# Reordering the first output projection of a two-block kernel, and issuing S5's transfers from GpSimd's queue

## The chip, the cores and the metric

One core of one Trainium2 chip runs the whole program. The metric is device time in microseconds, the median of three executions: 3645.99 us for the kernel before (3644.5 to 3646.58).

## The reference, cut to what matters

Two transformer-like blocks run on 256 tokens of width 2048, in float32. The change touches only the first half of the first block:

```
z = rmsnorm(x) @ w_in;  q, k, v, o, gates, u = split(z)
q, k = silu(causal_conv4(q, k))
hm = headnorm(mlstm(q, k, v, gates)) * g * sigmoid(o)     # 4 heads of 256: 1024 columns
ys = s5(u)             # 64 groups of 16 with a complex state of 64, gelu, 16x32 matrix per group, gate
x  = x + concat(hm, ys) @ w_out                           # 2048 x 2048
```

The S5 part is computed in chunks of 8 tokens: taps (the 8 by 8 kernel of a chunk), inputs (what a chunk adds to the state), a scan over 32 chunks, and outputs (state part plus taps part). The rest of the kernel (a PEER layer, then the second block) is untouched.

## The kernel before, in words

Every matrix product (`gemm`, L247 to L276) streams its weights from HBM: SyncE's queue loads 512 KB into `raw` (L238, 4 buffers), ScalarE writes the rounded high part `wh` (L247), VectorE the rest `wl` (L248), and TensorE does three matmuls for each block of 128 rows and each half of the tokens (L274 to L276) into a pair of PSUM banks `g`. There are four `g` banks, so two tiles of 512 columns are open at once. A second PSUM pool of four banks, `b`, serves all small products and transposes (L308 is the transposing helper).

Side work is written as Python generators in three queues (`side`). After each raw load, `gemm` calls `step`, which advances each queue by `steps` yields. Queue 0 holds S5, queue 1 the gates, heads 0 and 2 of mLSTM and the output gate `fin`, queue 2 heads 1 and 3. So the program order of S5 against the big product is set by counting yields. The tile framework then schedules each engine's stream by a model of its own, with program order as the priority; buffers are handed out by pool.

`phase_a` runs the stage. The first three column tiles of `w_in` give u and the gates, with one step for each of their 18 loads; S5's parameters (12 yields) and its first taps (7 yields) use them up but for one step. Then come eight tiles of 512 columns with 8 loads each and two steps a load, 16 steps a tile: v, q, k, output gate for heads 0 and 1 (half 0), then the same for half 1. The callback of a v tile copies it out to `V1` (L806, one buffer), that of a q or k tile copies it to `ev` (L813, two buffers), transposes it through `b` banks, copies it into `zp` (L815, one buffer) and convolves it (ACT L820, VectorE L822), then applies SiLU (L824). After k of a half its two heads are queued.

S5 (`s5_all`) takes, in steps: 5 for `s5_put_u` (u goes to DRAM and comes back regrouped as `U`, 8 transfers of 128 KB, L497), 7 for each of three further `s5_taps`, 4 for each of four `s5_in`, 15 for `s5_states` (the scan on GpSimd, L540 to L543), 6 for each of four quarters of `s5_out` (it begins by loading the quarter's taps, 1 MB, from DRAM into the only `s5t0` buffer, L554; its matmuls are L576 and L582; it draws two `b` banks in its fifth step and one in its sixth), and 8 for each `s5_glu`, which follows one quarter later (8 writes to DRAM at L599, one read back as `yT` at L603, six yields, then two steps with a `b` bank and two matmuls L610 each). All those transfers are on SyncE's queue, among the raw loads.

After the eight tiles, `w_out` runs in two passes of four column tiles: first its rows 1024 to 2047 against S5's half (`mix[1]`, in the buffers `s5t0` and `s5b`), adding to X; then, after draining the side queues, rows 0 to 1023 against mLSTM's half (`mix[0]` in `s5q`, filled by `mix_hm`), adding to X, transposing X into `xh` and `xl` for the next stage (`put_T`) and storing it.

```python
            self.gemm("w_out", [512] * 4, KD, *mix[1], cb_1, steps=2, ks=(8, 16))
            self.drain()
            self.gemm("w_out", [512] * 4, KD, *mix[0], cb_2, ks=(0, 8))
```

Of the kernel before, what the change touches and what calls it, by code (L numbers as in the profile page):

```python
# [11 lines left out]
F32 = mybir.dt.float32  # L12
F32R = mybir.dt.float32r
# [136 lines left out]

class Kern:
    def __init__(self, tc, A, ctx):
        self.tc, self.nc, self.A, self.ctx = tc, tc.nc, A, ctx
        self.side = [[], [], []]
        self.GB, self.heads = {}, set()
        self.raw_slots, self.raw_n = [None], 0
        self.half_step = []
# [22 lines left out]
    def drain(self, qs=(0, 1, 2)):  # L180
# [170 lines left out]
    def s5_params(self, p):  # L351
# [86 lines left out]
        nc.sync.dma_start(self.Kd.rearrange("q h s c -> (q h) s c")[:, 0:7, :],  # L438
# [4 lines left out]
    def s5_taps(self, p, q):  # L443
# [38 lines left out]
        nc.sync.dma_start(dr.rearrange("p g o -> p (g o)"), self.A["s5d"][:, q * 256:(q + 1) * 256])  # L482
# [3 lines left out]
        nc.sync.dma_start(bass.AP(tensor=k.tensor, offset=k.offset + q * 16 * 3840 + 7 * 256,  # L486
# [3 lines left out]
    def s5_put_u(self, p, uT):  # L490

        nc = self.nc
        ud = self.dram.tile([8, 128, 256], F32, name="ud")
        nc.sync.dma_start(ud.rearrange("n p x -> p n x"), uT.rearrange("p n j c -> p n (j c)"))
# [52 lines left out]
    def s5_out(self, p, q, yg):  # L547
# [4 lines left out]
        t0 = p.tile([128, 8, 16, 16], F32, name="s5t0")  # L552
        k = self.Kd
        nc.sync.dma_start(t0.rearrange("p i g o -> p (i g o)"),  # L554
                            bass.AP(tensor=k.tensor, offset=k.offset + q * 16 * 3840,
                                    ap=[[256, 8], [3840, 16], [1, 2048]]))
# [35 lines left out]
    def s5_glu(self, p, q, yg, ys):  # L592

        nc, V = self.nc, self.nc.vector
# [23 lines left out]
    def s5_all(self, p, uT, ys):  # L618
        yield from self.s5_put_u(p, uT)
        self.glu = p.tile([128, 8, 2, 128], F32, name="s5c")  # L620
        self.nc.sync.dma_start(self.glu.rearrange("p a b c -> p (a b c)"), self.A["glu"])
# [124 lines left out]
    def phase_a(self):  # L746
        nc, V, A = self.nc, self.nc.vector, self.A
        with ExitStack() as ex:
# [46 lines left out]
            def cb(i, P):  # L795
# [29 lines left out]
                if kind:  # L825
                    for h in range(2):
                        self.add_side(self.mlstm_head(mp, half * 2 + h, cur[1], cur[2], cur[0], hm), 1 + h)

            def fin(half, og):
                while not {2 * half, 2 * half + 1} <= self.heads:  # L830
                    yield
                for tb in range(2):
                    z = hm[tb][:, half * 512:(half + 1) * 512]
                    V.tensor_tensor(z, z, og[:, tb], op=OP.mult)
                yield
# [3 lines left out]
            X = [self.xx.tile([128, D], F32, name=f"X{tb}") for tb in range(2)]  # L839
            for tb in range(2):  # L840
                nc.sync.dma_start(X[tb], A["x"][tb * 128:(tb + 1) * 128, :])
            xh = self.act.tile([128, KD, T], F32R, name="xh")
            xl = self.act.tile([128, KD, T], F32R, name="xl")
            mix = [[s5.tile([128, 8, T], F32R, name=n, bufs=2 if n == "s5q" else 1) for n in nn]
                   for nn in (("s5q", "s5q"), ("s5t0", "s5b"))]
            for q in range(4):
                k, y = slice(2 * q, 2 * q + 2), ys[:, 2 * q:2 * q + 2]
                h, l = (z[:, k] for z in mix[1])
                nc.scalar.activation(h, y, AF.Copy)
                V.tensor_tensor(l, y, h.bitcast(F32), op=OP.subtract)  # L850

            def mix_hm():
                for q in range(2):
                    for tb in range(2):
                        z = hm[tb][:, q * 512:(q + 1) * 512]
                        b = self.transpose4([z[:, n * 128:(n + 1) * 128] for n in range(4)])
                        t = slice(tb * 128, tb * 128 + 128)
                        for n in range(4):
                            k = q * 4 + n
                            g = self.vecs[:, 48 + k:49 + k]  # L860
                            bn = b[:, n * 128:(n + 1) * 128]
                            h, l = (z[:, k, t] for z in mix[0])
                            nc.scalar.activation(h, bn, AF.Copy, scale=g)
                            V.scalar_tensor_tensor(l, bn, g, h.bitcast(F32), op0=OP.mult, op1=OP.subtract)
                        yield
            self.add_side(mix_hm(), 1)


            ss = self.xx.tile([128, 2, 4], F32, name="mss")

            def cb_1(i, P):
                for tb in range(2):
                    xs = X[tb][:, i * 512:(i + 1) * 512]
                    V.tensor_tensor(xs, xs, P[tb], op=OP.add)

            def cb_2(i, P):
                cb_1(i, P)
# [886 lines left out]
```

## Time and profile before

| what | value |
|---|---|
| median of 3 executions | 3645.99 us |
| profiled execution, its own time | 3642.74 us |
| its span, first to last instruction | 3641.0 us |
| TensorE busy | 3562.5 us, 98% of the span |
| granted TensorE clock, mean | 0.992 of full speed |

A span is taken from the first to the last recorded instruction. "PE" is TensorE's matmuls, "PEld" its weight loads, DVE is VectorE, ACT ScalarE, POOL GpSimd, SP SyncE. A row's releaser, after the arrow, is what ended the idle time ahead of the instruction. A granted clock of 1.00 is 2.4 GHz, 0.5 is 1.2 GHz.

### The profile page before, as it was taken

To read this page: it belongs to the slowest core of one execution; us is meant where nothing else is said; L and a number is where in the kernel's file an instruction comes from. 1 tells how busy PE (TensorE), PEld (TensorE's weight loads), DVE (VectorE), ACT (ScalarE), POOL (GpSimd) and SP (SyncE) were. 2 spreads that over 40 slices of the span, in tenths; PEclk is the share of its full clock that TensorE was granted. 3 is DMA by queue.
4 is the path that set the end of the run, shared out by engine and by line. 5 is a ranking of instruction groups with operands and counts; after the bars stand their busy time and mean duration, and the time that the engine had idled before them with its cause. 6 is when DMAs were issued, how large, how long until landed. Compare 5 with 4: busy or idle time off the path is not lost.

```text
span 3641.0 us, 52884 instructions
## 1 busy us (share of the span) xinstructions
PE 3562.5 (98%) x17442; PEld 2957.0 (81%) x17442; DVE 2711.8 (74%) x5655; ACT 2010.5 (55%) x3511; POOL 485.4 (13%) x645
## 2 busy tenths in 40 slices
PE   9898999999999999999999999999999999999999
PEld 7676888788888788888888788888887888888888
DVE  8685779869999977777777877766777666666554
ACT  6455655555555555555555666774454555555443
POOL 1060000014455500001000100000111000000000
PEclk9998999999999999999999999999999999999999
DMA  7656555555555578888887555466886577776565
GB/s 208 179 166 152 184 176 178 180 180 172 177 166 167 168 256 287 284 287 319 288 284 261 182 168 158 146 202 202 285 294 217 163 231 226 233 227 217 188 195 162
DMA packets 228516, 766.07 MB, mean 210 GB/s; under 512 B 40529, under 2 KB 44497, under 8 KB 226193
## 3 DMA queue, kind: packets, MB, share of 16 engines
q1 hardware_dynamic: 197728, 647.89, 56.0%
q0 software_dynamic: 30512, 114.81, 10.0%
q8 instruction: 137, 2.24, 0.2%
q14 instruction: 139, 1.13, 0.1%
HBM read 753.23 MB, written 9.37 MB: 209 GB/s over the span
## 4 chain that ended last, share of the span: by engine, by line
PE 77%; DVE 2%; POOL 1%; DMA 1%; issue 1%; ACT 1%; DVEq 0%; ACTq 0%; POOLq 0%
PE g L276 18%; PE g L274 18%; PE g L275 18%; PE g L1115 3%; PE g L1117 3%; PE b L1116 3%; PE b L1115 3%; PE g L1116 3%; PE b L1117 3%; PE b L308 1%; PE b L1064 1%; DVE wl L248 0%; POOL e L1057 0%; PE b L1456 0%; DMA fg<-in_fg_row 0%
## 5 line engine op out<-in xcount | busy, mean ns | idle before, releaser
L247 ACT ACTIVATE wh<-raw 128x512 fp32r<-128x512 f32 (+2 forms) x2068 | 1290.3, 629 | 1273.4 <-PE g L275 656.3
L248 DVE TENSOR_TENSOR wl<-raw,wh 128x512 fp32r<-128x512 f32 (+2 forms) x2068 | 1436.0, 705 | 663.4 <-ACT wh L247 613.3
L274 PE MATMUL g<-wh,xl 128*128 128x512 f32 (+2 forms) x3296 | 1268.7, 385 | 16.3 <-ACT wh L247 10.3
L275 PE MATMUL g<-wh,xh 128*128 128x512 f32 (+2 forms) x3296 | 1263.1, 384 | 0.0
L276 PE MATMUL g<-wl,xh 128*128 128x512 f32 (+2 forms) x3296 | 1089.0, 386 | 10.4 <-DVE wl L248 10.4
L274 PEld LDWEIGHTS g<-wh,xl 128*128 128x128 f32 x3296 | 622.1, 189 | 137.4 <-ACT wh L247 11.6
L275 PEld LDWEIGHTS g<-wh,xh 128*128 128x128 f32 x3296 | 622.5, 189 | 117.2 <-issue 0.4
L276 PEld LDWEIGHTS g<-wl,xh 128*128 128x128 f32 x3296 | 610.9, 189 | 129.4 <-DVE wl L248 18.0
L1057 POOL TENSOR_TENSOR e<-e,t 128x256 fp32r<-128x256 f32 x128 | 125.2, 981 | 574.3 <-DVE e L1056 292.6
L1115 PE MATMUL g<-wh,uev 128*128 128x512 f32 x504 | 196.4, 390 | 1.8 <-DVE uev L1103 1.4
L1115 PE MATMUL b<-wh,uev 128*128 128x512 f32 x504 | 196.2, 389 | 0.0
L1116 PE MATMUL b<-wh,uev 128*128 128x512 f32 x504 | 196.1, 389 | 0.0
L1116 PE MATMUL g<-wh,uev 128*128 128x512 f32 x504 | 196.1, 389 | 0.0
L248 DVE TENSOR_TENSOR wl<-xh,wh 128x512 fp32r<-128x512 f32 x202 | 135.4, 688 | 67.3 <-ACT wh L247 27.2
L247 ACT ACTIVATE wh<-xh 128x512 fp32r<-128x512 f32 x202 | 127.8, 633 | 52.3 <-PE g L1116 37.6
L274 PE MATMUL g<-wh,fl 128*128 128x512 f32 (+1 forms) x440 | 154.4, 351 | 0.0
L275 PE MATMUL g<-wh,fh 128*128 128x512 f32 (+1 forms) x440 | 154.2, 351 | 0.0
L1117 PE MATMUL g<-wl,uev 128*128 128x512 f32 x504 | 147.5, 389 | 1.6 <-DVE wl L248 1.6
L1117 PE MATMUL b<-wl,uev 128*128 128x512 f32 x504 | 146.7, 389 | 0.0
L906 DVE SCALAR_TENSOR_TENSOR xl<-xl 128x1024 f32<-128x1024 f32 x116 | 141.4, 1219 | 6.8 <-DMA xl<-in_w_ada 6.7
L910 POOL DMA_DIRECT2D xl<-in_w_ada x116 | 61.5, 530 | 593.4 <-DVE xl L906 584.0
L276 PE MATMUL g<-wl,fh 128*128 128x512 f32 (+1 forms) x440 | 132.7, 348 | 0.0
(558 smaller groups left out, 4073.2 us busy)
## 6 DMA issues: line engine op xcount, KB each, us to landing
raw<-in_peer_u SPq DMA_DIRECT2D x256, 512.0 KB, 3.7
raw<-in_w_in SPq DMA_DIRECT2D x192, 512.0 KB, 3.7
raw<-in_w_ffn_in SPq DMA_DIRECT2D x176, 512.0 KB, 4.2
raw<-in_peer_v SPq DMA_DIRECT2D x130, 512.0 KB, 5.2
xl<-in_w_ada POOLq DMA_DIRECT2D x116, 512.0 KB, 5.9
xh<-in_peer_v SPq DMA_DIRECT2D x101, 512.0 KB, 5.0
raw<-in_w_ffn_out SPq DMA_DIRECT2D x88, 512.0 KB, 3.6
raw<-in_w_out SPq DMA_DIRECT2D x64, 512.0 KB, 4.0
```

What stands on the lines that cost most here:

```text
L247: nc.scalar.activation(h[:, :n], r, AF.Copy)
L248: nc.vector.tensor_tensor(l[:, :n], r, h[:, :n].bitcast(F32), op=OP.subtract)
L274: nc.tensor.matmul(o, xl[:, k - ka, t], hs, start=k == ka, stop=False)
L275: nc.tensor.matmul(o, xh[:, k - ka, t], hs, start=False, stop=False)
L276: nc.tensor.matmul(o, xh[:, k - ka, t], ls, start=False, stop=k == kb - 1)
L308: self.nc.tensor.transpose(p[:, i * 128:(i + 1) * 128], s, self.ident)
L906: self.tc.keep_in_program_order(nc.vector.scalar_tensor_tensor(r, r, 1.0, cr, op0=OP.mult, op1=OP.mult, accum_out=self.macc[:, 2 * m + hf: ...
L910: nc.gpsimd.dma_start(r, w[n * 128:(n + 1) * 128, cs])
L1057: E.tensor_tensor(o2[:, :, 1], f(o2[:, :, 0]), bc(f(self.wl), t), op=OP.mult)
L1115: nc.tensor.matmul(o, w[:, 1, t], h, start=i1 == 0, stop=False)
L1116: nc.tensor.matmul(o, w[:, 0, t], h, start=False, stop=False)
L1117: nc.tensor.matmul(o, w[:, 0, t], l, start=False, stop=i1 == 127)
```

## The change

`w_out` now runs in three passes: rows 0 to 511 (heads 0 and 1), rows 512 to 1023 (heads 2 and 3), then 1024 to 2047 (S5). The operands of the first pass (`cur["mix"]`) lie in the buffers `zp` and `ev`, which the convolution of half 1 uses before them; those of the second in the first half of `xh`; those of S5's in `s5t0` and `s5b`, filled inside `s5_all`. Filling the first two is a generator `mix`, the first in a fourth side queue. The first two passes add to `xp`, a copy of x in the buffer `xl`; eight ScalarE copies move it to X in the third pass. After the eight tiles only the fourth queue is drained, not S5's.

All S5 transfers (zeros and taps to DRAM, s5d, u out and back, the glu matrix, the taps' loads, the outputs' turn) and the loads of x go on GpSimd's queue. A quarter's taps are asked for right after the quarter before has been computed (`s5_load`), and the turn through DRAM (`s5_turn`) is asked for three yields ahead of the next quarter, with the matmuls of `s5_glu` after that quarter. `s5_glu` gives up its six yields.

```diff
@@ s5_params, s5_taps, s5_put_u, s5_all: six lines like this one
-            nc.sync.dma_start(U[j * 16:(j + 1) * 16], bass.AP(tensor=ud.tensor, offset=ud.offset + j * 32,
+            nc.gpsimd.dma_start(U[j * 16:(j + 1) * 16], bass.AP(tensor=ud.tensor, offset=ud.offset + j * 32,
...
+    def s5_load(self, p, q):
+        t0 = p.tile([128, 8, 16, 16], F32, name="s5t0")
+        k = self.Kd
+        self.nc.gpsimd.dma_start(t0.rearrange("p i g o -> p (i g o)"),
...
-    def s5_glu(self, p, q, yg, ys):
+    def s5_turn(self, q, yg):
...
-            nc.sync.dma_start(bass.AP(tensor=yd.tensor, offset=yd.offset + q * 65536 + i * 32,
+            nc.gpsimd.dma_start(bass.AP(tensor=yd.tensor, offset=yd.offset + q * 65536 + i * 32,
...
-        nc.sync.dma_start(yT, yd[2 * q:2 * q + 2].rearrange("n p x -> p n x"))
-        for _ in range(6):
-            yield
+        nc.gpsimd.dma_start(yT, yd[2 * q:2 * q + 2].rearrange("n p x -> p n x"))
+        return yT
@@ s5_all
+        t0 = self.s5_load(p, 0)
         yield from self.s5_states(p)
         yg = self.xx.tile([128, 64, 32], F32, name="X1")
+        yT = None
         for q in range(4):
-            yield from self.s5_out(p, q, yg)
+            yield from self.s5_out(p, q, yg, t0)
+            if q < 3:
+                t0 = self.s5_load(p, q + 1)
             if q:
-                yield from self.s5_glu(p, q - 1, yg, ys)
-        yield from self.s5_glu(p, 3, yg, ys)
+                yield from self.s5_glu(q - 1, yT, ys)
+            yT = self.s5_turn(q, yg)
+            for _ in range(3):
+                yield
+        self.ymix = [p.tile([128, 8, T], F32R, name=n) for n in ("s5t0", "s5b")]
...
+        for q in range(3):
+            for hf in range(2):
+                parts(hf * 4 + q)
+            yield
+        for _ in range(3):
+            yield
+        yield from self.s5_glu(3, yT, ys)
+        for hf in range(2):
+            parts(hf * 4 + 3)
+        yield
@@ phase_a, callback of a k tile
+                    if half:
+                        z = mp.tile([128, 4, T], F32R, name="zp")
+                        e = [mp.tile([128, 2, T], F32R, name="ev", bufs=2) for _ in range(2)]
+                        cur["mix"] = Parts(4, z), Parts(2, *e)
+                        self.add_side(mix(0, *cur["mix"]), 3)
@@ phase_a, after the eight tiles
-            while self.side[0]:
-                self.step()
+            self.drain((3,))
...
-                nc.sync.dma_start(X[tb], A["x"][tb * 128:(tb + 1) * 128, :])
+            xp = self.act.tile([128, 4, 2, 512], F32, name="xl")
...
+                    nc.gpsimd.dma_start(xp[:, i, tb], A["x"][tb * 128:(tb + 1) * 128, i * 512:(i + 1) * 512])
+            self.add_side(mix(1, xh[:, 0:4], xh[:, 4:8]), 1)
...
-            self.gemm("w_out", [512] * 4, KD, *mix[1], cb_1, steps=2, ks=(8, 16))
+            self.gemm("w_out", [512] * 4, KD, *cur["mix"], cb_1, steps=2, ks=(0, 4))
+            self.drain((1, 2))
+            self.gemm("w_out", [512] * 4, KD, xh[:, 0:4], xh[:, 4:8], cb_1, steps=2, ks=(4, 8))
             self.drain()
-            self.gemm("w_out", [512] * 4, KD, *mix[0], cb_2, ks=(0, 8))
...
+            self.gemm("w_out", [512] * 4, KD, *self.ymix, cb_2, steps=2, ks=(8, 16))
```

## Rows read from the trace of the kernel before

**Rows 1.** The page's first part: the span, and TensorE's line of busy times.

```profile
span 3641.0 us, 52884 instructions
...
PE 3562.5 (98%) x17442; PEld 2957.0 (81%) x17442; DVE 2711.8 (74%) x5655; ACT 2010.5 (55%) x3511; POOL 485.4 (13%) x645
```

**Rows 2.** Stretches: length; PE, PEld, DVE, ACT, POOL busy; granted clock; DMA share; GB/s.

```profile
80.00:101.00 21.00, 12.88 (x120) 10.05 (x118) 4.77 (x18) 6.24 (x15) 0.74 (x1) 0.92 1.22 182
...
269.00:346.00 77.00, 59.55 (x540) 46.18 (x540) 48.38 (x92) 40.70 (x69) 0.00 (x0) 0.84 0.68 165
346.00:449.00 103.00, 101.89 (x461) 82.35 (x462) 73.20 (x194) 61.33 (x131) 3.30 (x6) 0.98 0.54 165
```

**Rows 3.** TensorE's waits from 0 to 430 us: total, times, longest.

```profile
PE g L274 <- ACT wh L247: 10.6, 3, 8.8
PE b L576 <- DMA s5t<-Kd: 7.7, 2, 4.1
...
PE g L274 <- DVE s5b L850: 3.7, 1, 3.7
...
PE g L274 <- DVE s5q L864: 0.6, 1, 0.6
```

**Rows 4.** ScalarE's copies of q and k tiles (L813), by stretch.

```profile
220.00:250.00 30.00, 1.37 (x2) 1.00 0.54 173
250.00:315.00 65.00, 0.00 (x0) 0.92 0.67 164
```

**Rows 5.** TensorE's timeline, 200 to 341 us: start, duration, line.

```profile
200.87 1.04 PE L308 MATMUL b<-ident,ev 128*128 128x128 f32 x8
...
268.35 0.64 PE L576 MATMUL b<-s5t,X 128*32 128x128 f32 x16
...
283.10 1.08 PE L576 MATMUL b<-s5t,X 128*32 128x128 f32 x16 [4.13 <-DMA s5t<-Kd]
...
314.51 1.46 PE L610 MATMUL b<-e,s5c 128*128 128x256 f32 x6
315.81 0.60 PE L308 MATMUL b<-ident,ev 128*128 128x128 f32 x4
...
331.22 3.75 PE L610 MATMUL b<-e,s5c 128*128 128x256 f32 x8 [2.25 <-DMA e<-yd]
334.76 1.91 PE L308 MATMUL b<-ident,ev 128*128 128x128 f32 x8
336.33 0.68 PE L274 MATMUL g<-wh,s5b 128*128 128x512 f32 x1
...
340.56 1.97 PE L610 MATMUL b<-e,s5c 128*128 128x256 f32 x8 [1.00 <-DVE kT L822]
```

**Rows 6.** The same timeline, 352 to 449 us.

```profile
352.27 0.38 PE L308 MATMUL b<-ident,kT 128*128 128x128 f32 x2
...
407.97 0.60 PE L308 MATMUL b<-ident,hm 128*128 128x128 f32 x4
...
448.78 0.39 PE L274 MATMUL g<-wh,xl 128*128 128x512 f32 x1
```

**Rows 7.** VectorE's convolution of k, half 1, and copies to zp, 321 to 348 us.

```profile
L822 DVE SCALAR_TENSOR_TENSOR kT<-zp,vecs,kT 128x256 f32<-128x256 f32 x12 | 5.1, 477 | 0.0
...
L815 DVE COPY zp<-b 128x512 f32<-128x512 f32 x2 | 1.4, 686 | 0.1
```

**Rows 8.** SyncE's queue, timeline: start, time spent issuing, line.

```profile
79.08 12.54 SPq L497 DMA_DIRECT2D X<-ud  x8
...
270.83 0.62 SPq L554 DMA_DIRECT2D s5t<-Kd  x1
```

**Rows 9.** The page's part 5: what GpSimd spends on issuing a transfer.

```profile
L910 POOL DMA_DIRECT2D xl<-in_w_ada x116 | 61.5, 530 | 593.4 <-DVE xl L906 584.0
```

**Rows 10.** The transfers' issues with KB and median us to landing.

```profile
X<-in_x SPq DMA_DIRECT2D x2, 1024.0 KB, 8.6
...
X<-ud SPq DMA_DIRECT2D x8, 128.0 KB, 8.6
```

More of the change, by code (lines that the diff above doesn't have):

```diff
@@ L148, in tile, with __init__, __getitem__ @@
         return ap
+class Parts:
+    def __init__(self, n, *tiles):
+        self.n, self.tiles = n, tiles
+    def __getitem__(self, at):
+        p, k, t = at
+        return self.tiles[k // self.n][p, k % self.n, t]
 class Kern:
@@ L153, in __init__ @@
         self.tc, self.nc, self.A, self.ctx = tc, tc.nc, A, ctx
-        self.side = [[], [], []]
-        self.GB, self.heads = {}, set()
+        self.side = [[], [], [], []]
+        self.GB, self.heads, self.halves = {}, set(), set()
         self.raw_slots, self.raw_n = [None], 0
@@ L551, in s5_out @@
         ms = slice(8 * q, 8 * q + 8)
[L552 to L556, printed above, removed]
         G2 = p.tile([128, 2, 8, 8, 16], F32, name="s5q", bufs=2)
@@ L620, in s5_all @@
         self.glu = p.tile([128, 8, 2, 128], F32, name="s5c")
-        self.nc.sync.dma_start(self.glu.rearrange("p a b c -> p (a b c)"), self.A["glu"])
+        self.nc.gpsimd.dma_start(self.glu.rearrange("p a b c -> p (a b c)"), self.A["glu"])
         for q in range(4):
@@ L625, in s5_all, with parts @@
             yield from self.s5_in(p, q)
+        t0 = self.s5_load(p, 0)
         yield from self.s5_states(p)
         yg = self.xx.tile([128, 64, 32], F32, name="X1")
+        yT = None
         for q in range(4):
-            yield from self.s5_out(p, q, yg)
+            yield from self.s5_out(p, q, yg, t0)
+            if q < 3:
+                t0 = self.s5_load(p, q + 1)
             if q:
-                yield from self.s5_glu(p, q - 1, yg, ys)
-        yield from self.s5_glu(p, 3, yg, ys)
+                yield from self.s5_glu(q - 1, yT, ys)
[3 more added lines that the diff above has]
+        self.ymix = [p.tile([128, 8, T], F32R, name=n) for n in ("s5t0", "s5b")]
+        def parts(k):
+            y, (h, l) = ys[:, k], (z[:, k] for z in self.ymix)
+            self.nc.scalar.activation(h, y, AF.Copy)
+            self.nc.vector.tensor_tensor(l, y, h.bitcast(F32), op=OP.subtract)
+        for q in range(3):
[8 more added lines that the diff above has]
+        yield
     def mlstm_gates(self, p, gt):
@@ L834, in fin @@
                     V.tensor_tensor(z, z, og[:, tb], op=OP.mult)
+                self.halves.add(half)
                 yield
-            self.gemm("w_in", W_IN_TILES[3:], KD, xh, xl, cb, steps=2, base=off)
-            while self.side[0]:
-                self.step()
-            X = [self.xx.tile([128, D], F32, name=f"X{tb}") for tb in range(2)]
-            for tb in range(2):
-                nc.sync.dma_start(X[tb], A["x"][tb * 128:(tb + 1) * 128, :])
-            xh = self.act.tile([128, KD, T], F32R, name="xh")
@@ L843, in phase_a @@
[L843 to L865, printed above, removed]
@@ L866, in phase_a, with mix @@
-            self.add_side(mix_hm(), 1)
+            def mix(half, h, l):
+                while half not in self.halves:
+                    yield
+                for tb in range(2):
+                    z = hm[tb][:, half * 512:(half + 1) * 512]
+                    b = self.transpose4([z[:, n * 128:(n + 1) * 128] for n in range(4)])
+                    t = slice(tb * 128, tb * 128 + 128)
+                    for n in range(4):
+                        g = self.vecs[:, 48 + half * 4 + n:49 + half * 4 + n]
+                        bn = b[:, n * 128:(n + 1) * 128]
+                        hn, ln = h[:, n, t], l[:, n, t]
+                        nc.scalar.activation(hn, bn, AF.Copy, scale=g)
+                        V.scalar_tensor_tensor(ln, bn, g, hn.bitcast(F32), op0=OP.mult, op1=OP.subtract)
+                    yield
@@ L869, in phase_a @@
+            self.gemm("w_in", W_IN_TILES[3:], KD, xh, xl, cb, steps=2, base=off)
+            self.drain((3,))
+            xh = self.act.tile([128, KD, T], F32R, name="xh")
+            xp = self.act.tile([128, 4, 2, 512], F32, name="xl")
+            for i in range(4):
+                for tb in range(2):
+                    nc.gpsimd.dma_start(xp[:, i, tb], A["x"][tb * 128:(tb + 1) * 128, i * 512:(i + 1) * 512])
+            self.add_side(mix(1, xh[:, 0:4], xh[:, 4:8]), 1)
             ss = self.xx.tile([128, 2, 4], F32, name="mss")
@@ L872, in cb_1, with cb_2 @@
                 for tb in range(2):
+                    V.tensor_tensor(xp[:, i, tb], xp[:, i, tb], P[tb], op=OP.add)
+            def cb_2(i, P):
+                for tb in range(2):
                     xs = X[tb][:, i * 512:(i + 1) * 512]
                     V.tensor_tensor(xs, xs, P[tb], op=OP.add)
-            def cb_2(i, P):
-                cb_1(i, P)
                 self.put_T(X, xh, xl, self.vecs[:, 16:32], i)
@@ L882, in cb_2, with move @@
                     nc.gpsimd.dma_start(self.h1d[tb * 128:(tb + 1) * 128, i * 512:(i + 1) * 512], xs)
-            self.gemm("w_out", [512] * 4, KD, *mix[1], cb_1, steps=2, ks=(8, 16))
+            self.gemm("w_out", [512] * 4, KD, *cur["mix"], cb_1, steps=2, ks=(0, 4))
+            self.drain((1, 2))
+            self.gemm("w_out", [512] * 4, KD, xh[:, 0:4], xh[:, 4:8], cb_1, steps=2, ks=(4, 8))
             self.drain()
-            self.gemm("w_out", [512] * 4, KD, *mix[0], cb_2, ks=(0, 8))
+            X = [self.xx.tile([128, D], F32, name=f"X{tb}") for tb in range(2)]
+            def move():
+                for i in range(4):
+                    for tb in range(2):
+                        nc.scalar.activation(X[tb][:, i * 512:(i + 1) * 512], xp[:, i, tb], AF.Copy)
+                    yield
+            self.add_side(move())
+            xl = self.act.tile([128, KD, T], F32R, name="xl")
+            self.gemm("w_out", [512] * 4, KD, *self.ymix, cb_2, steps=2, ks=(8, 16))
             self.dump("d_ys", ys.rearrange("p a b -> p (a b)"))
```

19 lines of the change are left out of this document (12 added, 7 removed).

## The prediction

> **What bounds the kernel now.** I read the page's first part, then busy times by stretch, then TensorE's waits, then its timeline where the waits are. TensorE is busy for 98% of the span [rows 1], so only its holes and its slow clock can be won. They lie in two places that this change touches. From 80 to 101 us it is busy for 12.88 of 21 us, while the DMA engines are at 1.22 [rows 2]: its longest wait, 8.8 us, is for a weight block [rows 3] that stands on SyncE's queue behind eight issues of S5's u, 12.54 us long [rows 8]. From 269 to 346 us it is busy for 59.55 of 77 us at a granted clock of 0.84 [rows 2], so part of it at 1.2 GHz; it waits for taps (7.7 us in two waits) and for S5's operand (3.7 us) [rows 3]. The rest up to 449 us is dense: 101.89 of 103 us at 0.98 [rows 2]. That is the prize, some 25 us, if mLSTM's half can fill those holes.
>
> **What orders the work there.** The copies of the q tile of half 1 to `ev` were done before 250 us, with none from 250 to 315 [rows 4]. Yet the transposes that follow them ran at 315.81, right behind the glu matmuls of S5's quarter 1 (314.51), and those of k at 334.76, right behind quarter 2's (331.22) [rows 5]. Nothing but a `b` bank was missing. I read from this that the four banks go out in program order, and that S5's banks, asked for early and held until its chain arrives, keep mLSTM's behind them. So I count steps. S5 takes 43 before its scan (one left over from its first taps, 5 for u, 7 for each of three taps, 4 for each of four inputs), 15 for the scan; its outputs begin at step 59. Before, quarter 1's glu draws its banks at 91 and 92, quarter 3's output at 97 and 98; q's callback comes after 96 (six tiles of 16), k's after 112. That is the order seen. After the change output 3 takes steps 90 to 95 (banks at 94, 95), glu 2 steps 96 and 97, glu 3 steps 107 and 108. **q of half 1 now stands behind S5's output 3, where it stood behind glu 1; k behind glu 3's request.** And the first pass needs k's convolution finished, because its operand lies in `zp`, which that convolution reads.
>
> **The change part by part.** The sum is made against the profiled execution, 3642.7 us (span 3641.0 and 1.7 around it), 3.3 below the median.
>
> *u through GpSimd's queue.* SyncE's weight loads get past it, so up to 8.8 us of wait and some slow clock disappear at 92 us. I count nothing for it: v of half 1 cannot be copied out before heads 0 and 1 leave `V1`, these follow k of half 0, whose transposes ran at 200.87 behind S5's input 3 [rows 5]; the product only meets the chain earlier. The bound is -9. What counts is when U is complete, for S5 starts there. Now the last issue ends at 91.6 and lands 8.6 us later [rows 8, 10]. On GpSimd an issue costs 0.53 us [rows 9], 4.2 us for eight against 12.54; but that row moves 128 long rows, and a load of U is 1024 pieces of 128 bytes. By pieces it would be 8 x 0.53 = 4.2 us each, 34 us for eight, U 21 us later. The engines were full in that stretch and must now carry weights as well. Bounds -4 and +21; I take **+2**, nearest to the row on the engines' share, which says that the data and not the issue set the pace.
>
> The Trainium skill, "DMA: Bandwidth & Descriptors", section "Issuing engines are not separate DMA queues", speaks against this part: transfers of all issuers run on the same 16 engines, and another issuer saves only the issue time. By it this term would be about 0, and the share of 1.22 agrees; my sum keeps +2.
>
> *S5's outputs.* Output 0 starts at 268.35 [rows 5], when the scan on GpSimd ends; that scan moves no DMA and stays. There is one `s5t0` buffer, so asking earlier still means asking after the quarter's last taps matmul, 2.5 us into it (issue at 270.83 [rows 8]). From there to the next output's first matmul is 12.3 us (283.10 [rows 5]). Three periods of 15 put output 3 at 313. Bounds: the free 1 MB load of 8.6 us [rows 10] and 2.5 give 11 and 302; before, the four quarters from output 0 to glu 3 (340.56 [rows 5]) took 18 each, giving 322.
>
> *From output 3 to the first pass.* Its two halves 3.6 us (two taps and two state groups as at 268.35), evacuation 0.4, q's transposes 0.6, copies to `zp` 1.4, ScalarE's first product 0.4, convolution 12 x 0.48 = 5.7 [rows 7]; the same copies and convolution for k, 7.5; `mix`'s transposes and first pieces, with hand-overs, 2.4 (estimated). Sum 22. The first pass starts at **335**, before 336.3 [rows 5]; bounds 324 and 344.
>
> *From there to the end of w_out.* Before, 336.3 to 448.8 [rows 5, 6], 112.5 us, of which 1.0, 3.7 and 0.6 were waits [rows 3, 5]: 107 of work, which stays: the same matmuls, the heads, glu 3, the transposes. New is a wait between passes one and two. Heads 2 and 3 took from 352.27 to 407.97, 55.7 us, eight hand-overs of TensorE some 5.5 us apart (it does weight matmuls between them) and 11.6 us of normalising. The first pass is 96 matmuls, 22 us, with 5 of the heads' own: about five hand-overs. Three are left at 2 us (estimated from busy times with nothing between), the 11 and 1.5 for the first pieces: 18.5, of which some 6 are TensorE's own work. So **+12**, bounded by 0 and 25; and **+3** for matmuls at 1.2 GHz after the two pauses (0 to 6, from the clock of 0.84 over 77 us).
>
> *The remainder* I cost at nothing: eight more additions to `xp` of 0.7 us on VectorE, eight copies of 0.6 us on ScalarE and eight loads of x on GpSimd lie beside 66 us of dense matmuls; if that cover is gone, up to 5 us. GpSimd's waits for a turn through DRAM hold the next taps' load behind them; that is inside the 15.
>
> Sum: 335 + 107 + 12 + 3 + 2 = 459, against 448.8: **10 us later**, 3652.7 for the execution, **3656** for the median, 0.3% slower.
>
> **The rivals.** *The chain gets quick:* taps land in 8.6 us, U four us earlier: output 3 at 298, first pass at 320, and with the wait and the clock as above 442, 7 us earlier. With a point or two less it is no change; 3639 to 3653. For it: 14 us of the old periods went to waits. Against: one buffer, and 12.3 us in the quietest quarter.
>
> *The banks don't bind* (on the other side): q and k of half 1 go when their copies are made, the first pass starts when the eight tiles end, about 292 (at 268 one tile, 20 us, was left, and output 0), and S5's outputs run inside it. 292 + 107 + 15 + 17 (three outputs and three glu that come after) = 431, 18 us earlier, **3628**. It decides if k's transposes run before S5's output 2. Against it: the two 60 us delays of rows 4 and 5. The change then does what its order says; by my forecast mLSTM's half isn't ready first.
>
> *GpSimd issues by the piece:* U 21 us late instead of 2, everything behind it 19 later, and the outputs' turn, 8 writes of 256 pieces, likewise slower: **3675**. For it: nothing in this trace has so many pieces on that queue. The Trainium skill, "SBUF — State Buffer", section "Who interferes with whom", adds a rule to the same effect: VectorE's copies in a two-port mode keep GpSimd from writing descriptors. No run here shows it yet; the 530 ns of rows 9 were issued beside VectorE's work without it.
>
> **How the numbers follow.** A difference under 0.2%, 7 us, can't be told from no change by a measurement of this kernel. Forecast 0.43 (its own range 3648 to 3666; 0.10 of it within 7 us), quick chain 0.27 (0.19 within, 0.08 faster), banks don't bind 0.18, issue by the piece 0.12. Faster 0.26, same 0.29, slower 0.45. The range reaches from the faster rival, a little beyond, to just short of the slow one: 3624 to 3672.
>
> **What would show it.** Right: k's transposes after S5's output 3, the first L274 on `ev` and `zp` at 325 to 345, a pause of TensorE of some 10 us ahead of the second pass, waiting for VectorE or ScalarE on heads 2 and 3, and no pause ahead of the third. The wait at 92 us gone, with tile 7 no earlier for it. Wrong: k's convolution before 300 us, or the second pass following at once.

## The result, and the profile after

The changed kernel takes 3681.11 us (median of 4 executions, 3677.66 to 3682.39) beside 3645.62 us of the kernel before on the same chip: the ratio is 1.0098, with a 95% interval of 1.0085 to 1.0112. It is slower, as forecast, but by 35 us where 10 were forecast, and outside the range. The profiled execution took 3682.39 us. The page's first part, where [rows 1] had 3641.0 and 98%:

```profile
span 3680.6 us, 52947 instructions
...
PE 3576.1 (97%) x17442; PEld 2965.0 (81%) x17442; DVE 2714.8 (74%) x5667; ACT 2016.0 (55%) x3523; POOL 529.4 (14%) x712
```

The stretches of [rows 2], same columns:

```profile
80.00:101.00 21.00, 16.81 (x141) 13.57 (x139) 9.95 (x25) 11.88 (x24) 8.08 (x11) 1.00 1.04 220
...
269.00:346.00 77.00, 55.03 (x534) 42.16 (x532) 34.11 (x67) 32.32 (x56) 28.56 (x53) 0.82 0.64 160
346.00:449.00 103.00, 82.85 (x331) 65.59 (x332) 71.06 (x197) 56.32 (x115) 1.89 (x3) 0.85 0.33 101
```

From 346 to 449 us TensorE was busy for 101.89 us and is now for 82.85, at a lower clock. The holes were not filled; new ones follow them. TensorE's waits, 0 to 500 us, beside [rows 3]:

```profile
PE b L628 <- DMA e<-yd: 19.7, 3, 12.7
PE b L529 <- DMA X<-ud: 7.7, 1, 7.7
PE b L319 <- ACT kT L865: 7.0, 1, 7.0
PE b L591 <- DMA s5t<-Kd: 4.8, 1, 4.8
```

The first is new in size: the turned quarter (yd to e), for which TensorE waited 2.9 us before:

```profile
PE b L610 <- DMA e<-yd: 2.9, 2, 2.2
```

TensorE's timeline in the changed kernel, the S5 outputs (L591), glu (L628), the transposes of q and k of half 1 (L319 on `ev`) and `w_out` (L285 on `ev`, then on `s5b`; the last row is the first matmul behind it):

```profile
270.15 0.64 PE L591 MATMUL b<-s5t,X 128*32 128x128 f32 x16
...
286.00 0.85 PE L591 MATMUL b<-s5t,X 128*32 128x128 f32 x16 [4.80 <-DMA s5t<-Kd]
...
310.02 0.64 PE L591 MATMUL b<-s5t,X 128*32 128x128 f32 x16
...
329.38 3.75 PE L628 MATMUL b<-e,s5c 128*128 128x256 f32 x8 [12.70 <-DMA e<-yd]
333.06 1.08 PE L591 MATMUL b<-s5t,X 128*32 128x128 f32 x16
...
340.81 1.95 PE L628 MATMUL b<-e,s5c 128*128 128x256 f32 x4 [1.85 <-DMA e<-yd]
342.55 1.91 PE L319 MATMUL b<-ident,ev 128*128 128x128 f32 x8
...
350.52 3.75 PE L628 MATMUL b<-e,s5c 128*128 128x256 f32 x8 [5.20 <-DMA e<-yd]
354.07 1.28 PE L319 MATMUL b<-ident,ev 128*128 128x128 f32 x8
...
365.00 0.69 PE L319 MATMUL b<-ident,kT 128*128 128x128 f32 x2 [6.96 <-ACT kT L865]
365.64 0.79 PE L285 MATMUL g<-wh,ev 128*128 128x512 f32 x1
...
435.46 0.39 PE L285 MATMUL g<-wh,s5b 128*128 128x512 f32 x1
...
482.87 0.39 PE L285 MATMUL g<-wh,xl 128*128 128x512 f32 x1
```

Output 3 starts at 333.06 (forecast 313, bounds 302 and 322), k is transposed at 354.07 behind glu 3, the first pass starts at 365.64 (forecast 335), and `w_out` ends at 482.87 against 448.78 [rows 6]: 34 of the 39.6 us by which the span grew. The other 5.5 lie behind `w_out`, where nothing was changed; in the runs below that remainder (span less the end of `w_out`) lies between 3190.2 us (outputs_40_u_5_sync, 3639.0 less 448.83) and 3197.3 (taps_on_sync, 3682.2 less 484.91), and here it is 3197.7, so such differences come without any edit there; I take it for scatter.

### The profile page after: what moved, and what is told of

Read it like the earlier page. It is cut to its first block, busy times and chain, and to the rows that moved or that the text cites. A ratio compares the mean times of both kernels' runs of the same rounds, so it can differ in the third digit from the quotient of the medians.

```text
span 3680.6 us, 52947 instructions
## 1 busy us (share of the span) xinstructions
PE 3576.1 (97%) x17442; PEld 2965.0 (81%) x17442; DVE 2714.8 (74%) x5667; ACT 2016.0 (55%) x3523; POOL 529.4 (14%) x712
## 3 DMA queue, kind: packets, MB, share of 16 engines
q0 software_dynamic: 34976, 127.86, 11.5%
## 5 line engine op out<-in xcount | busy, mean ns | idle before, releaser
L286 PE MATMUL g<-wh,xh 128*128 128x512 f32 (+2 forms) x3328 | 1279.3, 385 | 0.0
L285 PE MATMUL g<-wh,xl 128*128 128x512 f32 (+2 forms) x3296 | 1269.4, 386 | 9.5 <-DVE xl L359 5.2
L287 PE MATMUL g<-wl,xh 128*128 128x512 f32 (+2 forms) x3328 | 1102.4, 387 | 11.9 <-DVE wl L259 11.8
L285 PEld LDWEIGHTS g<-wh,xl 128*128 128x128 f32 x3296 | 622.8, 189 | 131.8 <-ACT wh L258 5.8
L286 PEld LDWEIGHTS g<-wh,xh 128*128 128x128 f32 x3328 | 630.5, 189 | 119.5 <-issue 0.5
L287 PEld LDWEIGHTS g<-wl,xh 128*128 128x128 f32 x3328 | 618.8, 190 | 133.4 <-DVE wl L259 19.6
L285 PE MATMUL g<-wh,fl 128*128 128x512 f32 (+1 forms) x440 | 154.4, 351 | 0.0
```

The lines of the kernel that those rows point to most:

```text
L285: nc.tensor.matmul(o, xl[:, k - ka, t], hs, start=k == ka, stop=False)
L286: nc.tensor.matmul(o, xh[:, k - ka, t], hs, start=False, stop=False)
L287: nc.tensor.matmul(o, xh[:, k - ka, t], ls, start=False, stop=k == kb - 1)
```

## The experiments

Two things stand against each other: the order in which the parts are written out, and the queue. The ratios are all to the kernel before, on the same chip as the run. This table holds what the traces gave: when output 3, the second transposes on `ev` (k) and the first matmul of `w_out` start and the last one ends, in us (in the two kernels with the order of before, the first pass is S5's half).

| kernel | output 3 | k | first pass | end | ratio, 95% |
|---|---|---|---|---|---|
| before | 322.31 | 334.76 | 336.3 | 448.8 | 1 |
| changed | 333.06 | 354.07 | 365.6 | 482.9 | 1.0098 (1.0085 to 1.0112) |
| all_on_sync | 322.82 | 345.79 | 356.9 | 472.8 | 1.0067 (1.0050 to 1.0084) |
| before_on_gpsimd | 329.91 | 348.92 | 337.1 | 461.4 | 1.0045 (1.0031 to 1.0059) |
| glu3_after_k | 330.89 | 344.18 | 359.3 | 480.1 | 1.0077 (1.0062 to 1.0093) |
| outputs_after_heads | 379.68 | 274.93 | 295.2 | 451.4 | 1.0024 (1.0014 to 1.0034) |
| after_heads_on_sync | 370.20 | 272.48 | 292.7 | 442.9 | 0.9993 (0.9983 to 1.0002) |

### The queue

**all_on_sync**: the ten statements that issue S5's transfers and the loads of x, all like this one:

```diff
-        self.nc.gpsimd.dma_start(t0.rearrange("p i g o -> p (i g o)"),
+        self.nc.sync.dma_start(t0.rearrange("p i g o -> p (i g o)"),
```

> The changed kernel with all its S5 transfers and the eight x loads back on SyncE's queue; order untouched. Theory A (order: the outputs' banks stand ahead of q's and k's of half 1 in program order, and the first pass waits for k's convolution, whatever the queue): the outputs' starts move by less than 5 us in all, the first pass still starts after 355, 3670 to 3680 us. Theory B (queue: output 3 came at 333 and not at 313 because the turned quarter's load, yd to e, stands on GpSimd's queue behind the 1 MB taps load and the x loads): PE's 19.7 us of waits for yd to e go for the most part, output 3 starts near 313, the first pass near 345, 3653 to 3662 us.

Measured 3666.98 us, ratio 1.0067; output 3 at 322.82, first pass at 356.9. Neither theory came out whole: output 3 came 10 us earlier, where A had less than 5 and B 20, and the time lies between the two. The queue costs 0.0031 of 3645, 11 us; the first pass is still past 355, and the other two thirds of the loss stay with the queue put back.

**before_on_gpsimd**: the kernel before with the same statements turned the other way (nine of them; its loads of x stay).

> The kernel before with its S5 transfers on GpSimd's queue as in the change; order of taps, outputs and w_out untouched. Theory A: the queue costs little by itself, within 3643 to 3650 us. Theory B: the turns and taps come later than over SyncE's queue, the outputs' period grows from about 15 us towards 20, and the half that is taken last stands behind them: 3655 us or more.

Measured 3656.48 us, 1.0045: theory B. With the source's order untouched the queue costs 16 us.

**u_on_sync**: only `ud` and its eight loads go back to SyncE.

> The changed kernel with only u's transfers (ud and its eight loads) on SyncE's queue. By the prediction's term for u (2 us, and the hole of PE near 92 us only moves): PE's wait for u (7.7 us) goes, a wait of 8 to 9 us for wh near 92 us comes back, output 0 within 2 us of 270, ratio 1.008 to 1.010. Rival (u on GpSimd's queue holds up more than its own landing): ratio 1.006 or less.

Measured 3677.67 us, 1.0093 (1.0077 to 1.0108), not to be told from the change itself: output 0 at 267.51, and TensorE's hole changes its owner. Output 0 is no measure of the term's 2 us, for in x_on_sync, with u on GpSimd's queue, it started at 267.35. TensorE's timeline in this run:

```profile
101.78 0.80 PE L285 MATMUL g<-wh,xl 128*128 128x512 f32 x1 [7.57 <-ACT wh L258]
```

The same timeline in the changed kernel:

```profile
104.53 1.08 PE L529 MATMUL b<-s5x,X 128*32 128x128 f32 x16 [7.72 <-DMA X<-ud]
```

There, the group of U's eight issues on GpSimd (busy in all, mean ns of one):

```profile
L508 POOL DMA_DIRECT2D X<-ud x8 | 6.1, 772 | 5.4 <-DMA ud<-s5c 5.4
```

And their time to landing, where [rows 10] had 8.6:

```profile
X<-ud POOLq DMA_DIRECT2D x8, 128.0 KB, 12.4
```

With U on SyncE a weight block is late by 7.6 us; with U on GpSimd the weights come, and TensorE stands 7.7 us for U itself.

### What makes the turned quarter late

**x_on_sync** moves the loads of x alone, **taps_on_sync** the taps (`s5_load`) alone, **bulk_on_sync** both, **turn_on_sync** the turned quarter (`s5_turn`, yd and e) alone, each by the edit above.

> The changed kernel with only the eight x loads (2 MB) on SyncE's queue. Theory A: no change, 3678 to 3683 us. Theory B: the wait of 12.7 us for yd to e ahead of output 3, whose load was asked between x loads at 316.1 and landed near 329, shrinks to under 5 us; output 3 starts near 325, and the time falls by 5 to 10 us, to 3671 to 3676 us.

> The changed kernel with only the four 1 MB taps loads (Kd to s5t) on SyncE's queue. Theory B1 (on GpSimd's queue a turned quarter's load, yd to e, stands behind the 1 MB taps load asked for just ahead of it: 12.8 us to land): PE's waits for yd to e fall from 19.7 us to under 8, ratio to before 1.005 to 1.008, as with everything on SyncE (1.0067). Theory B2 (it is GpSimd's issuing as such, 0.6 to 0.7 us an issue, 8 issues a turn, that is slow): ratio stays at 1.009 to 1.010.

> The changed kernel with the four 1 MB taps loads and the eight x loads on SyncE's queue together; turns (yd, e), u and the rest stay on GpSimd's. Theory B1 (a turned quarter waits behind whichever bulk load was put on its queue ahead of it: taking away the taps alone left the x loads, and the x loads alone left the taps): PE's waits for yd to e fall under 9 us and the ratio to 1.005 to 1.008. Theory B2 (GpSimd's issuing as such): waits over 15 us, ratio 1.009 or more.

> The changed kernel with only the turned quarter's transfers (yd and e, 9 per quarter) on SyncE's queue; taps, x and u stay on GpSimd's. If the turn is late because it shares a queue with the bulk loads (3 MB asked for between output 1 and output 3): output 3 starts at 321 to 326, PE's waits for yd to e fall under 10 us, ratio 1.005 to 1.008. If it is late because the bulk loads share the 16 DMA engines with it, whatever the queue: output 3 at 327 or later, waits over 15 us, ratio 1.008 or more.

Measured 1.0096 (1.0079 to 1.0113), 1.0091 (1.0074 to 1.0108), 1.0077 (1.0061 to 1.0092) and 1.0088 (1.0072 to 1.0103), with output 3 at 328.24, 335.99, 326.66 and 326.93. By their medians no one of them gives back what all together do, but the intervals overlap (that of bulk_on_sync both with the change's and with all_on_sync's), so the ratios don't decide here; the waits do. Theory B of x_on_sync and B1 of the other two fell: TensorE still waited 20.8 us for the turned quarter with x on SyncE, 27.0 with the taps and 20.2 with both, and with the turn alone on SyncE 23.3 us; in all_on_sync it was 7.9. The second reading of turn_on_sync, shared engines, has its wait and its ratio, with output 3 at its edge; B2 has the ratio of taps_on_sync, and the runs after these decide about it. What the runs share is in the time of the issues. GpSimd's queue in the changed kernel, start and time spent issuing:

```profile
305.47 4.61 POOL L614 DMA_DIRECT2D yd<-X  x8 [13.67 <-ACT X L604]
312.73 0.62 POOL L562 DMA_DIRECT2D s5t<-Kd  x1 [2.65 <-PE b L591]
315.44 0.59 POOL L907 DMA_DIRECT2D xl<-in_x  x1 [2.10 <-PE g L286]
316.11 0.73 POOL L618 DMA_DIRECT2D e<-yd  x1
```

SyncE's queue in the kernel before:

```profile
306.42 0.38 SPq L603 DMA_DIRECT2D e<-yd  x1
307.56 0.60 SPq L554 DMA_DIRECT2D s5t<-Kd  x1
```

The same queue in all_on_sync:

```profile
298.02 7.38 SPq L614 DMA_DIRECT2D yd<-X  x8
...
307.08 0.38 SPq L618 DMA_DIRECT2D e<-yd  x1
308.19 0.60 SPq L562 DMA_DIRECT2D s5t<-Kd  x1
```

In these two the turned quarter 1 is asked for ahead of the megabyte of taps, and glu 1 follows 7.4 and 7.5 us after the issue. TensorE's timeline before, then in all_on_sync:

```profile
313.79 0.67 PE L610 MATMUL b<-e,s5c 128*128 128x256 f32 x2 [0.63 <-DMA e<-yd]
```
```profile
314.58 1.10 PE L628 MATMUL b<-e,s5c 128*128 128x256 f32 x4 [1.23 <-DMA e<-yd]
```

In the changed kernel it stands behind the taps, which waited for output 2's matmuls, and behind a load of x, which waited for matmuls of the last tile: it is asked for 9 to 10 us later and takes 13.3 us. Not all of the later asking comes from those two: the turn's stores (yd) had themselves begun 7.5 us later than in all_on_sync, mostly for a reason told in the last section. The longer way stays without the later asking. In x_on_sync the turned quarter is asked for only 2 us later than in all_on_sync, but 0.7 us behind the taps, and glu 1 follows 15.3 us after the issue. GpSimd's queue and TensorE's timeline in that run:

```profile
309.22 0.74 POOL L618 DMA_DIRECT2D e<-yd  x1
```
```profile
324.55 3.75 PE L628 MATMUL b<-e,s5c 128*128 128x256 f32 x8 [12.07 <-DMA e<-yd]
```

In turn_on_sync the taps are asked for 1.2 us ahead of it on the other queue, and glu 1 follows 15.7 us after its issue. SyncE's queue in that run:

```profile
305.95 0.38 SPq L618 DMA_DIRECT2D e<-yd  x1
```

GpSimd's queue there:

```profile
304.71 0.58 POOL L562 DMA_DIRECT2D s5t<-Kd  x1 [15.80 <-PE b L591]
```

And TensorE's timeline:

```profile
321.64 3.75 PE L628 MATMUL b<-e,s5c 128*128 128x256 f32 x8 [10.94 <-DMA e<-yd]
```

So another queue doesn't take it past the bulk. The Trainium skill, "DMA: Bandwidth & Descriptors", section "Issuing engines are not separate DMA queues", says that transfers of all issuers interleave on the same 16 engines; the trace agrees, with 15.7 us beside the taps against 7.5 ahead of them. taps_on_sync had no taps ahead on GpSimd's queue but all eight loads of x, and asked for e only at 325.30; its trace puts the last 6.0 us ahead of that issue down to a load of x that had not landed yet.

**x_after_glu3** holds the loads of x back, and **x_after_glu3_taps_cut** also cuts the taps' bytes:

```diff
+                    V.tensor_copy(xp[:, i, tb, 0:1], ys[:, 7, 0:1])
                     nc.gpsimd.dma_start(xp[:, i, tb], A["x"][tb * 128:(tb + 1) * 128, i * 512:(i + 1) * 512])
```
```diff
+        n = 256 if q > 1 else 2048
-        self.nc.gpsimd.dma_start(t0.rearrange("p i g o -> p (i g o)"),
+        self.nc.gpsimd.dma_start(t0.rearrange("p i g o -> p (i g o)")[:, :n],
...
-                                         ap=[[256, 8], [3840, 16], [1, 2048]]))
+                                         ap=[[256, 8], [3840, 16], [1, n]]))
...
-                                 U[:, g, :], t0[:, :, g, :],
+                                 U[:, g, :], t0[:, :, g, :] if q < 2 else t0[:, 0:1, g, :].to_broadcast([128, 8, 16]),
```

> The changed kernel with the eight x loads held back until glu 3 is done, by a copy of 128 elements from its result into each load's destination; all on GpSimd's queue as changed, e of quarter 1 still behind the 1 MB of taps. If bytes ahead of e make it late: one of the two bulk loads is gone, glu 1's wait falls from 12.7 to some 6 to 9 us, output 3 starts at 325 to 330. The x loads now stand behind glu 3, near 352, and land by 365, ahead of the first use near 375, so they cost nothing: ratio 1.007 to 1.009. Rival (the queue's own issuing): wait unchanged, output 3 at 333.

> As x_after_glu3, and the taps loads of quarters 2 and 3 cut to an eighth (128 KB, one shift of eight, read eight times over by the same matmuls): it leaves out seven eighths of the taps of those quarters. If bytes ahead of e make it late: glu 1's wait falls under 4 us and output 3 starts at 318 to 323, ratio 1.004 to 1.007. Rival (the queue's own issuing, or PE's order): output 3 at 327 or later, ratio 1.008 or more.

Measured 3673.23 us, 1.0081 (1.0064 to 1.0098), with output 3 at 328.71; and 3666.02 us, 1.0060 (1.0043 to 1.0077). In the first, glu 1 still waited 10.7 us, where 6 to 9 were expected: without the loads of x the turned quarter was asked for 4.5 us earlier (311.64; 2.3 of it because its stores began earlier) and took 13.5 us, as before. So x held at most the asking, and what makes the way long is the taps. The second is as fast as everything on SyncE, with the queue as changed. Its GpSimd queue:

```profile
309.22 0.62 POOL L563 DMA_DIRECT2D s5t<-Kd  x1 [1.06 <-PE b L592]
310.75 0.74 POOL L619 DMA_DIRECT2D e<-yd  x1 [0.91 <-DMA yd<-X]
```

And TensorE's timeline in it:

```profile
315.48 1.89 PE L629 MATMUL b<-e,s5c 128*128 128x256 f32 x8
317.30 0.65 PE L592 MATMUL b<-s5t,X 128*32 128x128 f32 x16
```

The turned quarter is still behind the taps, but behind 128 KB of them: glu 1 runs 4.7 us after the issue without a wait, and output 3 starts at 317.30. The bytes asked for ahead of the turned quarter made its way long, not GpSimd's issuing; in the changed kernel the eight stores even take less time to issue there (4.61 us) than on SyncE's queue in all_on_sync (7.38). Part of the gain of this run is that output 3's own taps land sooner: all_on_sync waited 4.7 us for them, this run did not wait.

### The order

**glu3_after_k** gives k of half 1 a place ahead of glu 3:

```diff
-        for _ in range(3):
+        for _ in range(15):
             yield
         yield from self.s5_glu(3, yT, ys)
```

> The changed kernel with 15 idle steps in place of 3 ahead of glu 3, so that k of half 1 is written out ahead of it; queues as changed. Theory A (k's transposes stood right behind glu 3 at 354 because its banks come after glu 3's): k's transposes move to behind glu 2, some 8 to 12 us earlier, the first pass starts near 355, ratio 1.006 to 1.008. Rival (k waits for something else, its evacuation or the convolution's engines): first pass stays near 365, ratio 1.009 to 1.010.

Measured 3673.58 us, 1.0077. TensorE's timeline:

```profile
340.76 1.91 PE L319 MATMUL b<-ident,ev 128*128 128x128 f32 x8
...
344.18 1.13 PE L319 MATMUL b<-ident,ev 128*128 128x128 f32 x8
...
359.26 0.80 PE L285 MATMUL g<-wh,ev 128*128 128x512 f32 x1
```

k's transposes come 9.9 us earlier, with no other edit (counted from output 3, 13.3 us instead of 21.0): they were held by glu 3's place in the order. The first pass follows output 3 by 28.4 us instead of 32.6; the rest of its 6 us is that output 3 itself was 2 us earlier. So only 4.2 of the 7.7 us arrive: from k to the first pass it takes 15.1 us instead of 11.6, as k's copy to the one `zp` comes only behind q's convolution, which reads it (350.77). The ratio's interval overlaps that of the change. Which part of the order holds k, its place among the `b` banks or its place in TensorE's own stream, which follows the same order, is not shown: the edit moves both.

**outputs_after_heads** puts idle steps ahead of all the outputs, **outputs_30_later** 30 of them:

```diff
         yield from self.s5_states(p)
+        for _ in range(54):
+            yield
         yg = self.xx.tile([128, 64, 32], F32, name="X1")
```

> The changed kernel with 54 idle steps between the scan and S5's outputs in S5's side queue, so that q, k and the heads of half 1 are written out ahead of the outputs and take banks first; nothing else is changed. Theory A: q and k of half 1 are convolved near 280, the first pass starts right behind tile 7, below 325, the outputs run inside the first two passes, and the time falls to 3635 to 3655 us. Theory B: the outputs' period stays over 20 us wherever they stand, so the third pass waits for quarter 3 till 415 or later: 3655 to 3672 us.

> As outputs_after_heads with 30 idle steps in place of 54: q of half 1 is written out behind output 0's turn, k behind output 1, output 3 behind the heads. Theory A (the first pass starts when k's convolution is done, and k's bank stands behind the outputs that are written out ahead of it): first pass near 310 (two outputs of some 16 us and k's convolution, from 270), ratio 1.001 to 1.005. Theory B (the outputs' period alone decides): ratio as with 54, within 0.001 of 1.0024.

Measured 3649.62 us, 1.0024, and 3644.89 us, 0.9997 (0.9985 to 1.0009). TensorE's timeline in the first:

```profile
274.93 1.04 PE L319 MATMUL b<-ident,ev 128*128 128x128 f32 x8
...
295.15 0.50 PE L285 MATMUL g<-wh,ev 128*128 128x512 f32 x1 [1.92 <-DVE ev L899]
```

k is transposed 79 us earlier than in the change and the first pass starts 70 us earlier, with no edit but the order: theory A. The time falls by only 27 us, because outputs 1 to 3 now run behind the first pass and the heads (342.15, 357.00, 379.68), with 8.3 us of waits for turned quarters; the third pass starts at 396.4, with glu 3 at 404.8 inside it. With 30 steps the first pass starts at 322.4, behind three outputs, and one output is left over (360.4): better balanced, and level with the kernel before. I had put its first pass near 310.

### Looking for a kernel that beats both

**after_heads_on_sync** has both edits (54 steps, all on SyncE), **outputs_40_later_sync** 40 steps, **outputs_46_sync** 46. **outputs_30_bulk_sync** has 30 steps and the taps and x on SyncE, **outputs_30_u_5_later** also five idle steps behind `s5_put_u`; **outputs_40_u_5_sync** has 40 steps, those five, and only u on GpSimd.

> 54 idle steps and all S5 transfers and x loads on SyncE's queue. If order and queue cost separately (27 us and 11 us by the ratios 1.0096 to 1.0024 and 1.0067), the ratio is 0.999 to 1.000, level with the kernel before. If the queue only matters where the outputs stand ahead of the first pass, it stays at 1.001 to 1.003.

> 40 idle steps and all S5 transfers and x loads on SyncE's queue: outputs 0 and 1 start ahead of the first pass, outputs 2 and 3 behind the heads. Theory A: first pass near 300, less left over for the drain behind the second pass than with 54: ratio 0.996 to 1.000. Theory B: outputs 2 and 3 and their turns still end after 415, ratio over 1.000.

> 30 idle steps ahead of the outputs, taps and x loads on SyncE's queue. If the bulk loads delay turns there too: outputs_30_later's 0.9997 falls to 0.996 to 0.998. If PE's stream of weight matmuls covers the turns: 0.999 to 1.001.

> As outputs_30_bulk_sync, and 5 idle steps behind u's transfers, so that the first matmul on u comes some 9 us later in PE's stream. If u's landing near 104.5 is what PE waits for (8.6 us in outputs_30_later): that wait goes, and the ratio is 0.002 under that of outputs_30_bulk_sync. If the wait was hiding that of the scan behind it, the two ratios are level.

> All S5 transfers and x loads on SyncE's queue and 46 idle steps: k of half 1 is written out behind output 0, output 1 falls inside the first pass, output 2 behind the heads. Theory A: first pass near 305, end of w_out near 440, ratio 0.995 to 0.999. Rival (output 0 ahead of k costs as much as with 40 steps, first pass 324): 1.000 or more.

> u on GpSimd's queue with 5 idle steps behind it, the other S5 transfers and x loads on SyncE's, 40 idle steps ahead of the outputs: k behind output 0, output 1 inside the first pass. Theory A: first pass near 308, PE's hole at 80 to 105 us gone, ratio 0.994 to 0.999. Rival (as in outputs_30_u_5_later the 5 steps only delay the scan): 1.000 or more.

Measured 0.9993 (0.9983 to 1.0002), 1.0003 (0.9993 to 1.0013), 1.0005 (0.9996 to 1.0014), 1.0017 (1.0007 to 1.0026), 0.9998 (0.9989 to 1.0007) and 0.9999 (0.9990 to 1.0008). In the first, order and queue cost separately and add up, as expected. In the other five the gain that was hoped for did not come: with 40 steps the first pass started at 323.9 and not near 300, with 46 and with 40 and u's five steps it started where theory A had it (301.8, 305.2), and the time stayed level all the same. Against 30 steps on GpSimd alone, moving the bulk gave nothing. The five steps took away TensorE's wait for U (80 to 105 us: busy for 25.00 of 25 instead of 17.39 in outputs_30_bulk_sync), and the run was no faster: from 105 to 300 us TensorE was busy for 180.71 us instead of 187.27, so most of it was given back on the way to the outputs. No version is faster than the kernel before by more than can be told; the best are level with it. From 269 to 400 us each of these six leaves TensorE idle for 17 us or more (17.2 in outputs_40_u_5_sync, 18.7 in after_heads_on_sync), as the kernel before did for 17.6; outputs_30_later left 14.4 and was no faster. As I read it, S5's four quarters and the chain of heads 2 and 3 both have to end there, and no placing tried covers both; why, was not settled.

## Why the prediction was wrong

**Where the forecast was short.** Its sum had `w_out` end at 459; it ended 24 us later. With U's 2 us in it, output 3 was forecast at 315 and came 18 us later; the way from there to the first pass was 10.6 longer; the rest was 4.8 shorter. The profiled execution was 5.5 longer still behind `w_out`, the difference named above.

**u through GpSimd's queue.** +2 was taken, and output 0 started 1.8 us later (270.15), but that is no proof: in the runs with u on GpSimd's queue and the order as changed it started anywhere from 267.35 to 270.15, with u on SyncE's (before, all_on_sync, u_on_sync) from 267.51 to 268.99. By the rule of the Trainium skill that was weighed there ("DMA: Bandwidth & Descriptors", section "Issuing engines are not separate DMA queues") the term would have been about 0; the starts of output 0 leave room for that, and u_on_sync, 1.0093 beside 1.0098, can't tell the two apart. The gain at 92 us was counted as 0, and from 80 to 105 us TensorE was busy for 17.28 us instead of 16.25; but it was to show as a hole that is gone, and the hole only moved to 96.8 to 104.5, now waiting for U.

**"Three periods of 15 put output 3 at 313" failed.** The periods were 15.9, 24.0 and 23.0. Part of it could be read in the trace of before: I took output 0 to output 1, the quietest quarter, and kept the mean of the four as a bound. Outputs 2 and 3 of the kernel before:

```profile
305.10 0.64 PE L576 MATMUL b<-s5t,X 128*32 128x128 f32 x16
...
322.31 0.64 PE L576 MATMUL b<-s5t,X 128*32 128x128 f32 x16 [3.60 <-DMA s5t<-Kd]
```

Its periods were 14.8, 22.0 and 17.2, and all_on_sync has the same ones (15.0, 21.8, 17.1): asking a quarter ahead shortens nothing, since the one `s5t0` buffer and the turn set the pace. That is 8 of the 18 (315 to 322.82). Of the other 10 (322.82 to 333.06), 6 are the last period (23.0 instead of 17.1), in which glu 1 waited 12.7 us for the turned quarter behind the taps. The remaining 4 were there before that wait (output 2 at 310.02 beside 305.74), and among the runs with the turn on that queue and the same order output 2 starts at 305.80 (bulk_on_sync) to 310.02: that part is open. The prediction wrote "GpSimd's waits for a turn through DRAM hold the next taps' load behind them; that is inside the 15". It was the other way round: the taps and x, standing ahead of it, hold the turn.

**"Sum 22" from output 3 to the first pass failed**: it measured 32.6. The order was read rightly, k behind glu 3, but I charged nothing for the glu matmuls that stand in between and wait for their own operand. q was summed 4.0 us behind output 3 and came 9.5 behind it (342.55), with the first half of glu 2 and its wait of 1.9 us for e ahead of it. From q to k the sum had 8.1 us and it took 11.5: I let k wait for glu 3's request alone, but glu 3 waited 5.2 us for e and ran at 350.52, and k followed at 354.07. From k on it took 11.6 us, against 9.9 in the sum. glu3_after_k shows glu 3's place: 13.3 us from output 3 to k instead of 21.0; of these 7.7 us, 4.2 reach the first pass.

One reading behind this was wrong. The prediction speaks of "the two 60 us delays": only q's copies stood that long. ScalarE's copies of k, half 1, in the kernel before:

```profile
317.16 0.69 ACT L813 ACTIVATE ev<-g,rA 128x512 f32<-128x512 f32 x1
```

They start right behind q's transposes (315.81), which read the two `ev` buffers, and k's transposes follow at 334.76: k waited for q's buffers first, and only the last 14 us can be a bank's.

**From the first pass to the end** 117.2 us were measured and 122 forecast: 107 of work, and 10 instead of 15 for heads 2 and 3 and the clock, if those 107 stayed. The pause lay where it was put but was shorter: from 392.0 to 404.4 us TensorE was idle for 4.1 us, where some 10 were forecast, at a granted clock of 0.78; the second pass started at 404.43, and the third followed without a pause.

**The rivals.** *The chain gets quick* was wrong: the old periods stayed (all_on_sync), and the turned quarter came on top. *The banks don't bind* was wrong for this kernel but right about the price of the order: with the order turned, the first pass started at 295.2, where that rival had 292. It put the end at 431 and the run had 451.4, as three outputs and the heads didn't all hide behind two passes. *GpSimd issues by the piece* named a time near the result, 3675, for a reason that the trace denies: an issue of 1024 pieces took 772 ns, not 4.2 us, and x_after_glu3_taps_cut gave the queue's part of the loss back with GpSimd's issues in place.

## What to carry to other kernels

A transfer that the next matmul waits for should be issued ahead of the bulk that is only wanted later: here 256 KB took 7.5 us from the issue to their first use ahead of a megabyte and 13 to 16 us behind one, on the same queue or the other. When parts share a few buffers and one stream of work in program order, the place in the program decides who waits, and moving a part costs what its slowest neighbour ahead of it waits for. Read every period of a repeated step, not the quietest one.

## What I had not expected

A queue's move changed the order on other engines. The first half of output 1 was ready by 289 in the changed kernel (288.80, the end of its state group) and by 287.08 in all_on_sync, but ScalarE in the changed one splits weight blocks first, which wait for TensorE. Its timeline:

```profile
295.08 0.63 ACT L258 ACTIVATE wh<-raw 128x512 fp32r<-128x512 f32 x1 [12.71 <-PE g L286]
...
299.14 0.64 ACT L601 ACTIVATE e<-b 128x256 f32<-128x256 f32 x2
```

In all_on_sync the same evictions (L601) ran as soon as TensorE was done:

```profile
287.08 0.38 ACT L601 ACTIVATE e<-b 128x256 f32<-128x256 f32 x1 [5.72 <-PE b L597]
290.07 0.38 ACT L601 ACTIVATE e<-b 128x256 f32<-128x256 f32 x1 [2.61 <-PE b L597]
```

So the turn of quarter 1 began at 305.47 instead of 298.02, with the same source but for the queue. It comes with the queue: counted from output 1's start, the turn began 18.6 to 20.0 us later in the eight runs with the order of outputs as changed and the turn on GpSimd's queue, and 13.4 and 14.0 us later in the two with the turn on SyncE's (turn_on_sync, all_on_sync). Why the queue changes ScalarE's order was read, not tried by itself; in x_after_glu3_taps_cut the turn began at 303.32 and output 3 was early all the same. Also unexpected: the 256 KB of e took 7.5 us ahead of a megabyte and 15.7 us just behind one on another queue.
